# The maxima of a matrix-memory recurrence: rows through DRAM and a GpSimd mask instead of two wide products

## The chip, the cores and the metric

The kernel runs on one core of one Trainium2 chip. The core has TensorE (PE, matrix products), VectorE (DVE), ScalarE (ACT), GpSimd (POOL), and SyncE (SP), which here issues every DMA of the kernel. The time is device time in microseconds of one launch. The kernel before takes 2779.44 us (median of three runs, 2777.0 to 2782.29).

## The reference

One layer of a streaming encoder over 2048 tokens with 1024 features, all in 32-bit floats:

```
xn = RMSNorm(x);  proj = xn @ w_in
A = band attention, 8 heads of 64, a chunk of 64 tokens sees itself and 8 chunks to its left
M = matrix-memory recurrence (mLSTM), 4 heads of 128
y = sigmoid(ga) * (A @ w_att) + sigmoid(gm) * (M @ w_mlstm);  x = x + y @ w_out
x = x + relu(RMSNorm(x) @ w_up)^2 @ w_down;  out = RMSNorm(x)
```

The change is in M. For each head there is a log forget gate, summed to `b_t`, an input gate `i_s`, and a running maximum `m_t` that keeps the exponentials in range. Inside a chunk the output of token t weighs the values of the tokens s up to t by

```
D[t, s] = exp(b_t - b_s + i_s - m_t)   for s <= t, else 0
num_t = sum_s (q_t . k_s) D[t, s] v_s + (what the memory carried so far gives)
```

With `u_s = i_s - b_s` and `mt_t = m_t - b_t` the weight is `exp(u_s - mt_t)`: one number of the key's token, one of the query's token. The kernel needs it as a matrix with s over the 128 partitions and t over the columns, so `u` is one number per partition, and `mt` must be there as the same row in every partition, together with a mask for s > t.

## The kernel before, in words

The tokens are in four blocks of 512 (`NB`), each four tiles of 128 (`NT`). A block keeps features over partitions and its 512 tokens along the columns. The large products, input projections, the two projections of A and M, and the feed-forward part, run at 128x512 with operands split in a high and a low part, three products for one (`mm3` at L642, or L727 and L755, where blocks of a product are combined Strassen-like). Everything that does not fit into SBUF goes through DRAM tensors: q, k, v, the recurrence's inputs (`mfar`, `mvfar`), its results (`mixd`), gates and partial sums.

Buffers come from pools: 28 `r` (128x2x512), 16 `ctx` and 6 `tmp` (both 128x516), eight PSUM banks, and a few more. The order of the work is made in two steps when the kernel is built. First, `Flow` runs each piece of work as a thread that asks for buffers, waits for events, and asks for time on an engine (`yield "pe", 440`); the thread that can start earliest by a model of costs goes next. The large products are one thread of their own, `dense`, with the lowest priority. Then `Order` takes all instructions with their dependences, simulates them again with costs and margins of its own, and fixes the sequence on each of the five queues. No instruction passes another one on its queue on the chip.

A block's recurrence goes through these places:

- `gates_rest` (L1500): small operations on 128x16 tiles, a column for each tile and head. A cumulative sum and a running maximum (made on 16 rows, after a transpose) give `u`, `mt` and the factors `ex`. At the end (L1585 to L1592) `mt` is transposed, tile by tile, into a bank as rows of 512 tokens, and ScalarE and VectorE keep it in `mtt` as a rounded part in rows 0 to 3 and a remainder in rows 32 to 35. This sets the event `gates`.
- `recurrence_far` (L1596): takes the buffers of a head (two heads may be under way, `N_REC`), and starts `load_rec` (k, q and the values from DRAM) and `rec_head`.
- `rec_head` (L1662): two wide products into one bank. The first (L1670) multiplies a 16-bit identity by a 16-bit mask and so writes the mask, -1e30 for s > t, under all four tiles. The second (L1671) adds `-mt`, the high and the low row, in every partition. Then four exponentials on ScalarE (L1675) add `u` and give the weights `w`. Next the keys are transposed (L1682) and scaled (L1686), q and k multiplied (L1693), and the product multiplied into `w` on VectorE (L1695). Four tiles in turn then give the outputs (L1707 to L1709) and bring the memory forward (L1712). A norm (its root on GpSimd, L1729), transposes (L1742) and the output gate end the head, and its result is stored.

There are four blocks with four heads each, 16 heads. GpSimd also fills the corners of attention's bias tiles (L1324, L1325) and finishes eight output gates (L1659). Rows that go through DRAM into all partitions exist already for the norms: `row_out` (L1117) transposes 128x4 numbers, copies them and stores 512 numbers; `row_in` (L1131) reads them with a partition step of zero, 256 KB.

Of the kernel before, what the change touches and what calls it, by code (L numbers as in the profile page):

```python
# [30 lines left out]
P = 128  # L31
D = 1024
S = 2048
T = 512
# [178 lines left out]
def act_ns(n, ps=False, ap=0):  # L213
    return (51 if ps else 93) + 0.834 * n + 93 * ap
# [158 lines left out]
class Layer:  # L373
# [8 lines left out]
    def make_tiles(self, pool, psum):  # L382
# [14 lines left out]
        self.ones = f32("ones", 2)  # L397
        self.identb = pool.tile([P, P], BF16, name="identb")
        self.maskb = pool.tile([P, 1, P], BF16, name="maskb")
        self.gw = f32r("gw", KT, 40)  # L400
# [7 lines left out]
        self.cst = [f32(f"cst{h}", 129) for h in range(MH)]  # L408
        self.mtt = f32r("mtt", T)
        self.nsel = f32r("nsel", 8)  # L410
        self.cum = [pool.tile([16, 192], F32, name=f"cum{i}") for i in range(2)]
# [25 lines left out]
    def setup_late(self):  # L437
# [11 lines left out]
        nc.vector.tensor_sub(self.gw[:, :, 32:40], gwr, self.gw[:, :, 0:8].bitcast(F32))  # L449
        nc.vector.memset(raw[:, :512], 0.0)  # L450
        nc.vector.tensor_copy(self.mtt, raw[:, :512])
        fl.put(self.temp, raw)
# [7 lines left out]
        nc.vector.tensor_copy(self.bif[:, 1:, :], self.bif[:, 0:1, :].to_broadcast([P, NT - 1, 8]))  # L460
        nc.vector.tensor_copy(self.identb, self.ident)
# [1038 lines left out]
    def gates_rest(self, b):  # L1500
# [83 lines left out]
        V.tensor_scalar(ex[:, 2], ex[:, 2], C1, None, op0=ALU.mult)  # L1584
        yield "pe", 428  # L1585
        for c in range(NT):
            nc.tensor.transpose(bk[:MH, c * P:(c + 1) * P], sm["mt"][:, c * MH:(c + 1) * MH], self.ident)
# [27 lines left out]
    def load_rec(self, b, h):  # L1615
# [46 lines left out]
    def rec_head(self, b, h):  # L1662
# [4 lines left out]
        yield "wait", [B["gates"]]  # L1667
        (bk,) = yield "get", self.banks, 1
        yield "pe", 440
        mm(bk.rearrange("p (c t) -> p c t", c=NT), self.identb, self.maskb.to_broadcast([P, NT, P]), start=True, stop=False)  # L1670
        mm(bk, self.nsel[:, h:h + 1].to_broadcast([P, P]), self.mtt, start=False, stop=True)  # L1671
        for c in range(NT):
            n = c * MH + h
            yield "act", act_ns(128, True, 1)
            nc.scalar.activation(w[:, c * P:(c + 1) * P], bk[:, c * P:(c + 1) * P], AF.Exp,  # L1675
                                 bias=self.sm["u"][:, n:n + 1])
        fl.put(self.banks, bk)
        yield "wait", [B["qk_ev"][MH + h]]
# [4 lines left out]
        for c in range(NT):  # L1683
            n = c * MH + h
            yield "act", act_ns(128, True, 1)
            nc.scalar.mul(kt[:, c * P:(c + 1) * P], bk[:, c * P:(c + 1) * P], ex[:, 2, n:n + 1])  # L1686
        fl.put(self.banks, bk)
        yield "wait", [B["qk_ev"][h]]
        (bk,) = yield "get", self.banks, 1
# [767 lines left out]
    def build(self):  # L2457
# [16 lines left out]
        self.ud = f32d("u", 4, 7, 4, P, T)  # L2474
        self.rowd = {n: f32d("row" + n, T) for n in ("in1", "in2", "in3", "mid0", "mid1", "mid2", "mid3", "out0", "out1", "out2")}
        self.wi = 0
        self.y3 = [{}, {}]
# [16 lines left out]
        for b in range(NB):  # L2494
            self.blk.append(dict(
                xs=[], xg=[], vs={}, xs_ev=Event(), xn=E(KT), xs_done=E(KT), x2=E(KT), v_slots=Event(), v_ev=E(NT), v_spilt=E(NT),
                kq_ev=E(AH), q_ev=E(AH), k_ev=E(AH), k_spilt=E(AH), kq_all=Event(), head_done=E(AH),
                gates=Event(), mv_slots=Event(), mv_ev=E(NT), ctx={}, mvh={}, ctx_ev=E(MH), qk_ev=E(2 * MH), og_ev=E(MH),
                mix=[None] * 8, mix_ev=E(8), ga={}, ga_ev=E(8), xs_free=Event(), x_room=E(KT), mid=Event(), vo={}, vn={}, vp_ev=E(4), mvh_ev=E(MH), gf=Event(), rec_slots={}, heads_left=[2] * 4))
# [94 lines left out]
```

## Time and profile before

| | |
|---|---|
| runs, median | 2779.44 us (2777.0 to 2782.29) |
| the profiled execution | 2782.55 us, its span 2780.8 us |
| TensorE, weight loads | 99%, 82% of the span |
| VectorE, ScalarE, GpSimd | 74%, 54%, 2% |
| DMA | 678.64 MB, mean 244 GB/s |

The span runs from the first to the last instruction. A busy share of TensorE counts a product from its issue to its modelled end, and products overlap, so what one product takes from the next is the distance between their starts. In a group's row, the number after the bar is the time in which at least one instruction of the group ran, then the mean of one in ns, then the engine's idle time just before the group and what ended it. In a timeline's row come the start, the duration, the engine (with a q for its sequencer, which issues DMAs), the line, the operation and the tiles. A row of waits has the total, the number and the longest.

### The profile page before, as it was taken

Reading aid. Unit: us, or ns where it says so; the run is one execution under the profiler, and the core shown is the slowest. Engines: PE = TensorE matmul, PEld = TensorE weight load, DVE = VectorE, ACT = ScalarE, POOL = GpSimd, SP = SyncE. Lnnn points to the kernel's source line nnn. Section 1 sums busy time; section 2 is a strip of 40 time slices with the busy share of each in tenths; the row PEclk is TensorE's granted clock in tenths of the full one; section 3 lists DMA queues with packets and bytes.
Section 4 is the critical chain, followed back from the end, with each engine's and each line's share of the span. In section 5 each row is a group of like instructions: output and inputs, shape, how many; then the busy total and the mean of one; then the engine's idle time right before and its main releaser. Section 6 shows DMA issues by size and latency. Waiting matters only on the chain.

```text
span 2780.8 us, 38634 instructions
## 1 busy us (share of the span) xinstructions
PE 2754.7 (99%) x13018; PEld 2288.4 (82%) x13018; DVE 2055.0 (74%) x3776; ACT 1493.2 (54%) x2608; POOL 52.6 (2%) x100
## 2 busy tenths in 40 slices
PE   9999999999999999999999999999999999999998
PEld 7888888888778888888888888888887888888887
DVE  7696789758995866886676688789888656555565
ACT  5564576544453535575556556566436655554443
POOL 0000001000000000000000000000000000000000
PEclk9999999999999999999999999999999999999999
DMA  7958759768764677588877887787877667776574
GB/s 267 294 190 283 230 164 310 248 223 314 261 206 171 235 255 257 194 273 325 288 281 269 286 245 232 231 256 255 248 251 261 208 222 263 239 238 220 190 227 151
DMA packets 329046, 678.64 MB, mean 244 GB/s; under 512 B 36840, under 2 KB 67728, under 8 KB 328848
## 3 DMA queue, kind: packets, MB, share of 16 engines
q1 hardware_dynamic: 328848, 676.18, 73.3%
q8 instruction: 102, 1.67, 0.2%
q14 instruction: 96, 0.79, 0.1%
HBM read 472.59 MB, written 203.44 MB: 243 GB/s over the span
## 4 chain that ended last, share of the span: by engine, by line
PE 88%; DVE 4%; DMA 4%; issue 2%; ACT 1%; SPq 0%; POOLq 0%; POOL 0%; DVEq 0%; ACTq 0%
PE bank L727 41%; PE bank L644 12%; PE bank L645 11%; PE bank L646 11%; PE bank L1415 2%; PE bank L1388 2%; PE bank L755 2%; PE bank L1446 2%; DVE wsp L585 1%; DMA ctx<-in_xt 1%; DMA qfar<-ctx 1%; PE bank L1707 1%; PE bank L1709 1%; PE bank L1708 1%; PE bank L1693 0%
## 5 line engine op out<-in xcount | busy, mean ns | idle before, releaser
L727 PE MATMUL bank<-r,wsp 128*128 128x512 f32 x5544 | 1266.4, 390 | 2.9 <-DVE ctx L2088 1.5
L727 PEld LDWEIGHTS bank<-r,wsp 128*128 128x128 f32 x5544 | 1037.5, 188 | 225.4 <-DVE ctx L1874 4.2
L585 DVE TENSOR_TENSOR wsp<-wraw,wsp 128x1024 fp32r<-128x1024 f32 x459 | 560.5, 1221 | 352.9 <-ACT wsp L583 343.2
L583 ACT CAST wsp<-wraw 128x1024 fp32r<-128x1024 f32 x459 | 482.1, 1051 | 449.5 <-PE bank L727 202.9
L644 PE MATMUL bank<-r,wsp 128*128 128x512 f32 x1472 | 586.0, 398 | 2.8 <-ACT r L1224 2.8
L645 PE MATMUL bank<-r,wsp 128*128 128x512 f32 x1472 | 574.8, 391 | 0.2 <-DVE r L1229 0.2
L646 PE MATMUL bank<-r,wsp 128*128 128x512 f32 x1472 | 574.8, 391 | 0.0
L646 PEld LDWEIGHTS bank<-r,wsp 128*128 128x128 f32 x1472 | 276.2, 188 | 58.8
L644 PEld LDWEIGHTS bank<-r,wsp 128*128 128x128 f32 x1472 | 276.7, 188 | 54.2 <-ACT r L1224 3.1
L645 PEld LDWEIGHTS bank<-r,wsp 128*128 128x128 f32 x1472 | 277.0, 188 | 50.5 <-DVE r L1229 0.5
L1874 DVE TENSOR_TENSOR ctx<-bank,ctx 128x512 f32<-128x512 f32 x186 | 127.0, 687 | 91.6 <-PE bank L727 91.4
L1229 DVE TENSOR_TENSOR r<-r 128x512 fp32r<-128x512 f32 x248 | 163.7, 686 | 27.3 <-ACT r L1224 26.3
L1224 ACT CAST r<-r 128x512 fp32r<-128x512 f32 x248 | 147.5, 624 | 57.1 <-DMA r<-u 53.3
L1866 ACT COPY ctx<-bank 128x512 f32<-128x512 f32 x186 | 107.8, 581 | 66.7 <-PE bank L727 65.2
L1430 ACT ACTIVATE sc<-sc,scs 128x640 f32<-128x640 f32 (+4 forms) x128 | 97.4, 762 | 73.3 <-DVE scs L1427 63.0
L2205 ACT ACTIVATE ctx<-ctx 128x512 f32<-128x512 f32 x96 | 60.6, 631 | 103.1 <-DVE ctx L1874 103.1
L1451 DVE TENSOR_TENSOR r<-bank,r 128x512 fp32r<-128x512 f32 (+1 forms) x168 | 96.9, 595 | 17.4 <-ACT r L1449 16.6
L1449 ACT CAST r<-bank 128x512 fp32r<-128x512 f32 (+1 forms) x168 | 81.5, 517 | 48.7 <-PE bank L1446 45.6
L1421 DVE CUSTOM_DVE_ANT_0 sc<-bank,bias 128x320 f32<-128x320 f32 (+3 forms) x240 | 103.4, 461 | 5.5 <-PE bank L1415 5.0
L1388 PE MATMUL bank<-r,r 128*128 128x512 f32 x336 | 95.3, 365 | 1.3 <-DVE r L1451 1.2
L602 DVE TENSOR_TENSOR wraw<-wraw,wraw 128x1024 f32<-128x1024 f32 x76 | 92.8, 1223 | 2.0
L552 DVE TENSOR_TENSOR ctx<-ctx,ctx 128x512 f32<-128x512 f32 x112 | 76.2, 686 | 13.8 <-DMA ctx<-in_wf 9.7
(258 smaller groups left out, 2721.3 us busy)
## 6 DMA issues: line engine op xcount, KB each, us to landing
wraw<-in_wf SPq DMA_DIRECT2D x178, 512.0 KB, 4.3
wraw<-wsum SPq DMA_DIRECT2D x136, 512.0 KB, 3.9
r<-u SPq DMA_DIRECT2D x224, 256.0 KB, 4.4
wraw<-in_w SPq DMA_DIRECT2D x88, 512.0 KB, 5.2
u<-ctx SPq DMA_DIRECT2D x128, 256.0 KB, 2.8
ctx<-in_wf SPq DMA_DIRECT2D x112, 256.0 KB, 4.2
wsum<-ctx SPq DMA_DIRECT2D x112, 256.0 KB, 3.8
u<-tmp SPq DMA_DIRECT2D x96, 256.0 KB, 3.5
```

What stands on the lines that cost most here:

```text
L583: nc.scalar.copy(w[:, 0], raw)
L585: nc.vector.tensor_sub(w[:, 1], raw, w[:, 0].bitcast(F32))
L644: mm(ps, lh, rh, start=first, stop=False)
L645: mm(ps, lh, rl, start=False, stop=False)
L646: mm(ps, ll, rh, start=False, stop=last)
L727: mm(ps, wv[:, x, k, n], a[:, y], start=new and k == 0 and x == y == 0, stop=k == 3 and x == 1, skip_group_check=True)
L1224: self.nc.scalar.copy(dst[:, 0], src)
L1229: self.nc.vector.tensor_sub(dst[:, 1], src, dst[:, 0].bitcast(F32))
L1388: nc.tensor.matmul(acc[:, :, c0:c0 + w], st, sl[:, :, o:o + w], start=n == 0, stop=n == total - 1)
L1421: nc.vector.tensor_tensor_reduce(out=e[:, x * w:x * w + w], in0=bks[x][:, :w], in1=br[:, j0 + x * w:j0 + x * w + w], op0=ALU.add, op1=ALU. ...
L1866: nc.scalar.copy(t[:, o:o + 512], ps)
L1874: nc.vector.tensor_add(t[:, o:o + 512], ps, t[:, o:o + 512])
```

## The change

`mt` no longer goes to `mtt`. VectorE copies it with heads ahead of tiles, one transpose makes 16 rows of 128, ScalarE copies these to SBUF, and SyncE stores them in a DRAM tensor `rowm` of the block. A new thread for each head, `row_rec`, reads the head's 512 numbers back into all partitions of `w`, and GpSimd adds `later`, a 128x128 mask of 0 and 1e30, under each of the four tiles. `rec_head` drops the two products, their bank, and the exponentials in front; it makes the exponentials behind the scaled keys, in place in `w`, with scale -1. `mtt`, `nsel`, `identb` and `maskb` go, and a seventh `tmp` buffer comes in.

```diff
-        self.temp = Pool([f32(f"tmp{i}", 516) for i in range(6)])
+        self.temp = Pool([f32(f"tmp{i}", 516) for i in range(7)])
...
-        nc.vector.tensor_scalar(self.maskb[:, 0], self.tri, 1.0, -NEG, op0=ALU.subtract, op1=ALU.mult)
-        nc.vector.tensor_scalar(self.nsel, self.sel, -1.0, None, op0=ALU.mult)
+        nc.vector.tensor_scalar(self.later[:, 0], self.tri, NEG, -NEG, op0=ALU.mult, op1=ALU.add)
...
-        yield "pe", 428
-        for c in range(NT):
-            nc.tensor.transpose(bk[:MH, c * P:(c + 1) * P], sm["mt"][:, c * MH:(c + 1) * MH], self.ident)
-        yield "act", act_ns(512, True)
-        nc.scalar.copy(self.mtt[:MH], bk[:MH])
-        yield "dve", dve_ns(512)
-        yield "dve", 85
-        V.tensor_sub(self.mtt[32:32 + MH], bk[:MH], self.mtt[:MH].bitcast(F32))
+        yield "dve", 85
+        V.tensor_copy(p.rearrange("p (m c) -> p m c", c=NT), v4("mt").rearrange("p c m -> p m c"))
+        yield "pe", 110
+        nc.tensor.transpose(bk[:16, 384:512], p, self.ident)
+        yield "act", act_ns(P, True)
+        nc.scalar.copy(z[:, 64:], bk[:16, 384:512])
         fl.put(self.banks, bk)
+        yield "sp", 900, 2000
+        nc.sync.dma_start(self.rowm[b].ap(), z[:, 64:])
         fl.set(B["gates"])
...
             fl.spawn(self.load_rec(b, h), 1)
+            fl.spawn(self.row_rec(b, h, B["ctx"][h][3]), 1)
             fl.spawn(self.rec_head(b, h), 1)
...
+    def row_rec(self, b, h, w):
+        fl, nc, B = self.fl, self.nc, self.blk[b]
+        yield "wait", [B["gates"]]
+        yield "sp", 900, 2000
+        nc.sync.dma_start(w[:, :T], bass.AP(self.rowm[b], h * T, [[0, P], [1, T]]))
+        yield "pool", 730
+        w4 = w[:, :T].rearrange("p (c t) -> p c t", c=NT)
+        nc.gpsimd.tensor_tensor(w4, w4, self.later.to_broadcast([P, NT, P]), op=ALU.add)
+        fl.set(B["row_ev"][h])
...
         yield "wait", [B["gates"]]
-        (bk,) = yield "get", self.banks, 1
-        yield "pe", 440
-        mm(bk.rearrange("p (c t) -> p c t", c=NT), self.identb, self.maskb.to_broadcast([P, NT, P]), start=True, stop=False)
-        mm(bk, self.nsel[:, h:h + 1].to_broadcast([P, P]), self.mtt, start=False, stop=True)
-        for c in range(NT):
-            n = c * MH + h
-            yield "act", act_ns(128, True, 1)
-            nc.scalar.activation(w[:, c * P:(c + 1) * P], bk[:, c * P:(c + 1) * P], AF.Exp,
-                                 bias=self.sm["u"][:, n:n + 1])
-        fl.put(self.banks, bk)
         yield "wait", [B["qk_ev"][MH + h]]
...
             nc.scalar.mul(kt[:, c * P:(c + 1) * P], bk[:, c * P:(c + 1) * P], ex[:, 2, n:n + 1])
         fl.put(self.banks, bk)
+        yield "wait", [B["row_ev"][h]]
+        for c in range(NT):
+            n = c * MH + h
+            yield "act", act_ns(128, False, 1)
+            nc.scalar.activation(w[:, c * P:(c + 1) * P], w[:, c * P:(c + 1) * P], AF.Exp, scale=-1.0,
+                                 bias=self.sm["u"][:, n:n + 1])
         yield "wait", [B["qk_ev"][h]]
```

More of the change, by code (lines that the diff above doesn't have):

```diff
@@ L397, in make_tiles @@
         self.ones = f32("ones", 2)
-        self.identb = pool.tile([P, P], BF16, name="identb")
-        self.maskb = pool.tile([P, 1, P], BF16, name="maskb")
+        self.later = f32("later", 1, P)
         self.gw = f32r("gw", KT, 40)
@@ L408, in make_tiles @@
         self.cst = [f32(f"cst{h}", 129) for h in range(MH)]
-        self.mtt = f32r("mtt", T)
-        self.nsel = f32r("nsel", 8)
         self.cum = [pool.tile([16, 192], F32, name=f"cum{i}") for i in range(2)]
@@ L2475, in build @@
         self.rowd = {n: f32d("row" + n, T) for n in ("in1", "in2", "in3", "mid0", "mid1", "mid2", "mid3", "out0", "out1", "out2")}
+        self.rowm = [f32d(f"rowm{b}", 16, P) for b in range(NB)]
         self.wi = 0
@@ L2497, in build @@
                 kq_ev=E(AH), q_ev=E(AH), k_ev=E(AH), k_spilt=E(AH), kq_all=Event(), head_done=E(AH),
-                gates=Event(), mv_slots=Event(), mv_ev=E(NT), ctx={}, mvh={}, ctx_ev=E(MH), qk_ev=E(2 * MH), og_ev=E(MH),
+                gates=Event(), mv_slots=Event(), mv_ev=E(NT), ctx={}, mvh={}, ctx_ev=E(MH), qk_ev=E(2 * MH), row_ev=E(MH), og_ev=E(MH),
                 mix=[None] * 8, mix_ev=E(8), ga={}, ga_ev=E(8), xs_free=Event(), x_room=E(KT), mid=Event(), vo={}, vn={}, vp_ev=E(4), mvh_ev=E(MH), gf=Event(), rec_slots={}, heads_left=[2] * 4))
```

3 lines of the change are left out of this document (removed).

## The prediction

> **What bounds the kernel now.** I read the page first (span, busy shares, granted clock, DMA queue), then the waits of TensorE, then its timeline at both ends and around the lines that the change touches.
>
> ```profile
> span 2780.8 us, 38634 instructions
> PE 2754.7 (99%) x13018; PEld 2288.4 (82%) x13018; DVE 2055.0 (74%) x3776; ACT 1493.2 (54%) x2608; POOL 52.6 (2%) x100
> PEclk9999999999999999999999999999999999999999
> q1 hardware_dynamic: 328848, 676.18, 73.3%
> ```
>
> TensorE (PE) is busy for 99% of the span at an undiminished clock. VectorE (DVE), ScalarE (ACT) and the DMA queue have a quarter or more left, and GpSimd (POOL) is all but unused. A high busy share can hide stalls, so I looked at what TensorE waited for:
>
> ```profile
> PE bank L644 <- ACT r L1180: 6.7, 1, 6.7
> PE bank L644 <- ACT r L1224: 2.8, 1, 2.8
> PE bank L1707 <- DMA r<-mvfar: 0.9, 1, 0.9
> ...
> 2770.67 1.13 PE L2435 MATMUL bank<-const,ctx 128*128 128x128 f32 x7
> ```
>
> The first wait, 6.7 us, is the start of the program. The last products end at 2770.67 + 1.13 = 2771.8 us, so 9.0 us are the tail. Of the 2780.8 - 2754.7 = 26.1 us without TensorE work, 26.1 - 6.7 - 9.0 = 10.4 us lie inside, the longest of them 2.8 us. In this kernel a TensorE instruction that disappears is time, unless something new makes TensorE wait.
>
> **The change part by part.** First the two wide products a head.
>
> ```profile
> L1671 PE MATMUL bank<-mtt,nsel 128*128 128x512 f32 x16 | 9.0, 583 | 0.0
> L1670 PE MATMUL bank<-maskb,identb 128*128 128x512 bf16 x16 | 6.2, 388 | 0.0
> ...
> 69.01 0.39 PE L646 MATMUL bank<-r,wsp 128*128 128x512 f32 x1
> 69.24 0.39 PE L1670 MATMUL bank<-maskb,identb 128*128 128x512 bf16 x1
> 69.28 0.58 PE L1671 MATMUL bank<-mtt,nsel 128*128 128x512 f32 x1
> 69.70 0.39 PE L1670 MATMUL bank<-maskb,identb 128*128 128x512 bf16 x1
> ...
> 70.16 0.39 PE L644 MATMUL bank<-r,wsp 128*128 128x512 f32 x1
> ```
>
> The groups' busy columns, 9.0 + 6.2 = 15.2 us, are not the saving: they hold each product from issue to modelled end, and products overlap (the ordinary one at 69.01 is listed with 0.39 us, yet the next starts after 0.23). What TensorE gives up is the distance between starts. Two heads run from 69.24 to 70.16, 0.92 us, so 0.46 us a head, and 16 heads give 7.4 us. I take starts because the neighbours are packed; the busy columns would be right only if TensorE did one product at a time, which these rows exclude.
>
> The maxima are also turned differently: four transposes of four columns a block become one of sixteen.
>
> ```profile
> 65.14 0.39 PE L646 MATMUL bank<-r,wsp 128*128 128x512 f32 x1
> 65.37 0.60 PE L1587 MATMUL bank<-const,g_mt 128*4 128x128 f32 x4
> ...
> 66.04 0.39 PE L645 MATMUL bank<-r,wsp 128*128 128x512 f32 x1
> ...
> 55.55 0.39 PE L646 MATMUL bank<-wsp,r 128*128 128x512 f32 x1
> 55.78 0.27 PE L1541 MATMUL bank<-const,g_u 128*16 128x128 f32 x1
> ...
> 56.12 0.39 PE L645 MATMUL bank<-wsp,r 128*128 128x512 f32 x1
> ```
>
> From the product before (65.14) to the second one after (66.04) are 0.90 us; two ordinary steps of 0.23 leave 0.44 for four transposes. L1541 has the shape of the new one: 0.57 less 0.46 is 0.11. Each block saves 0.33, four blocks 1.3 us. Together TensorE sheds 7.4 + 1.3 = 8.7 us.
>
> Now what is added. The rows below are the nearest to each step: a row read back from DRAM into all partitions (L1133, 256 KB, as here), a short row's copy and store (L1125, L1128), the only 128x512 GpSimd operation (L1659, one input where the new add has two), the k and q loads of a head (L1625), and an exponential from a bank (L1675) beside an activation from SBUF (L1761).
>
> ```profile
> L1125 ACT COPY tmp<-bank x10: 237/242/255, 180.7 to 2742.2; 4x128 f32<-4x128 f32 x10
> L1128 SPq DMA_DIRECT2D rowmid<-tmp x4: 265/270/305, 1358.7 to 2279.7; - x4
> L1133 SPq DMA_DIRECT2D tmp<-rowmid x8: 319/354/747, 1621.8 to 2688.3; - x8
> DMA to landing us min/median/max: 3.2/4.1/7.5
> ...
> L1659 POOL TENSOR_SCALAR ctx<-ctx,ghead x8: 902/1596/2022, 194.3 to 453.3; 128x512 f32<-128x512 f32 x8
> ...
> L1625 SPq DMA_DIRECT2D r<-mfar x32: 319/382/830, 135.5 to 1808.1; - x32
> DMA to landing us min/median/max: 3.3/6.0/8.2
> ...
> L1675 ACT ACTIVATE ctx<-bank,g_u 128x128 f32<-128x128 f32 x64 | 18.4, 378 | 5.8 <-PE bank L1671 5.8
> ...
> L1761 ACT ACTIVATE tmp<-tmp 128x128 f32<-128x128 f32 x64 | 19.9, 310 | 16.6 <-DVE tmp L1757 13.2 <-DVE ctx L2242 2.8 <-DVE r L1229 0.3
> ```
>
> *Queues.* SyncE issues 4 stores and 16 loads more, 4 x 0.27 + 16 x 0.35 = 6.7 us in all, and the loads add 16 x 0.26 = 4.2 MB to 676 MB (0.6%) on a queue at 73%. I cost both at nothing: TensorE's waits name DMA once, for 0.9 us. Without that cover each load would cost its issue, 0.35 us. The load behind a fresh store must wait until the store has landed, and whatever SyncE holds behind it (mostly weight and operand loads) waits too; by the landings of L1133 that is 3.2 to 7.5 us, four times at most, less what the planner puts between.
>
> *GpSimd.* 16 adds of 0.9 to 2.0 us, 14 to 32 us on an engine with 52.6 us of work. Queued behind them are the bias memsets of attention and the root of a head's norm; both have idle time before them. An add may also slow VectorE (third rival).
>
> *ScalarE.* 64 exponentials move behind the turned keys and read SBUF: at most 64 x (378 - 310) ns = 4.4 us less work, off the path, so nothing.
>
> *The setup and the spare buffer.* Some small VectorE work before 30 us goes. The seventh temporary buffer can only let loads start earlier; at best it removes part of the 10.4 us inside, and the new written order may equally make other waits. I take zero, with 10.4 us to either side as bounds.
>
> *The head's own chain* is the one term that can hurt. Before, the products needed only the gates; now a head needs load, add and exponentials before its weights (L1695), and TensorE needs these at L1707. A tight head, and (last two rows) the first heads of the last block, which start from fresh gates:
>
> ```profile
> 207.14 0.38 SPq L1625 DMA_DIRECT2D r<-mfar  x1
> 211.34 1.73 POOL L1659 TENSOR_SCALAR ctx<-ctx,ghead 128x512 f32<-128x512 f32 x1 [7.08 <-ACT ctx L1656]
> 214.90 1.14 ACT L1686 ACTIVATE ctx<-bank,g_ex 128x128 f32<-128x128 f32 x4
> 216.19 0.68 DVE L1695 SCALAR_TENSOR_TENSOR ctx<-bank,ctx 128x512 f32<-128x512 f32 x1
> 218.67 0.38 PE L1707 MATMUL bank<-r,ctx 128*128 128x129 f32 x2
> ...
> 1779.94 0.60 PE L1587 MATMUL bank<-const,g_mt 128*4 128x128 f32 x4
> ...
> 1796.49 0.41 PE L1707 MATMUL bank<-r,ctx 128*128 128x129 f32 x2
> ```
>
> Issued just behind the keys at 207.5, the row lands at 211.6 (4.1), waits for the operation on GpSimd to 213.1, is added by 214.7 (1.6), and its exponentials follow the scaled keys at 216.0 and take 1.2: 217.2. The weights then start 1.0 us later than now and end at 217.9, 0.8 us ahead of L1707. With the longest landing, 7.5, the row comes at 215.0, the add ends at 216.6, the exponentials at 217.8 and the weights at 218.5, still ahead by 0.2. With the longest add as well (2.0) TensorE waits 0.2 us, and where the other head's add stands ahead on GpSimd, 2.0 more. From fresh gates: turned at 1780.5, copy 0.24, store issue 0.27 and landing 4.1 (no row gives a short store's landing; I use the load's), load 0.35 and 4.1, add 1.6, exponentials of two heads 2.5, weights 0.7, so 1794.4, 2.1 us ahead of L1707. The bounds a head are thus 0 and some 2.2 us; I take 0.9 us in all, the one wait for a DMA at L1707 that TensorE shows among 16 such loads, since the planner lays other products in between in the same way.
>
> The sum on the profiled execution, which took 2782.55 us (its span 2780.8): 2782.55 - 8.7 + 0.9 = 2774.7. That execution lies 3.1 us above the median of the runs, 2779.44, so the forecast for the median is 2779.44 - 7.8 = 2771.6 us, 0.28% less.
>
> **The rivals.** *The order is planned anew and the gain is swallowed.* Every instruction behind the first gates is laid out again. If the 10.4 us inside become 10.4 + 7, the time is 2779.44 - 8.7 + 7 = 2777.7, no difference that can be told. For it: the inner idle is already so small that a new order is likelier to add to it than to take away. Against: the other work stays what it is, and the planner that now leaves 10.4 us of holes is the one that lays it out again.
>
> *Rows come late (the other side).* The place is L1707 (and L1693 ahead of it); the price is up to 2.2 us a head. It decides from 8.7 / 16 = 0.54 us a head on: at 1.2 us on average, 16 x 1.2 = 19 us, the time is 2779.44 - 8.7 + 19 = 2790. For it: load, add and exponentials now stand in a row, behind queues that hold other work. Against: 32 loads at L1625 that take up to 8.2 us never show in TensorE's waits, and 16 at L1707 once.
>
> *The adds hold VectorE off.*
>
> ```profile
> L1229 DVE TENSOR_TENSOR r<-r 128x512 fp32r<-128x512 f32 x248 | 163.7, 686 | 27.3 <-ACT r L1224 26.3
> ...
> 438.29 1.75 POOL L1659 TENSOR_SCALAR ctx<-ctx,ghead 128x512 f32<-128x512 f32 x1 [3.09 <-ACT ctx L1656]
> ...
> 439.48 1.10 DVE L1229 TENSOR_TENSOR r<-tmp,r 128x512 fp32r<-128x512 f32 x1
> ```
>
> This split, 0.69 us in the mean, took 1.10 beside the GpSimd operation that runs from 438.29 to 440.04. If TensorE waited for a whole add of 2.0 us each time, 32 us, the time would be 2779.44 - 8.7 + 32 = 2803. Against: VectorE is idle for a quarter of the span and all of TensorE's inner idle time is 10.4 us, so I expect 0.4 us of VectorE delay for an add, hidden. [...]
>
> **How the numbers follow.** About 0.2%, 5.6 us, is what a measurement of this kernel can tell from no change. The forecast, TensorE time saved and all or nearly all kept, has 0.62, with a range of its own from 2762 (8.7 saved and most of the inner idle gone) to 2773.8. Swallowed: 0.20. Late rows: 0.14; VectorE held off: 0.04. So faster 0.62, same 0.20, slower 0.18. The range for 8 in 10 leaves out the best tenth, and the worse half of the slower cases: 2762 to 2788.
>
> **What would show it.** TensorE's instructions fall by 32 + 12 to 12974 and its span time with them; L1670 and L1671 vanish, and no new wait on ScalarE's exponentials, on the weights of L1695 or on DMA appears in its waits with more than 1 us in total. GpSimd gains 16 operations of 0.9 to 2.2 us, DMA 4.2 MB. I am wrong if TensorE's idle time inside exceeds 10.4 us by over 3, above all at L1707 or L1693, or if bank or weight waits on VectorE grow near the adds.

## The result, and the profile after

The changed kernel takes 2794.92 us (median of six runs, 2790.74 to 2798.68) beside 2779.51 us of the kernel before (six runs). The ratio is 1.0056, with a 95% interval from 1.0045 to 1.0066: 0.56% slower, where 0.28% faster was forecast.

The head of the page of the changed kernel (span; busy time, share and instructions of each engine; DMA queue):

```profile
span 2792.7 us, 38602 instructions
PE 2753.1 (99%) x12974; PEld 2288.6 (82%) x12974; DVE 2055.9 (74%) x3772; ACT 1494.5 (54%) x2608; POOL 74.6 (3%) x116
q1 hardware_dynamic: 331280, 680.41, 72.2%
```

TensorE has the 44 instructions less that were forecast, GpSimd its 16 more, the queue its 4.2 MB more, at 72.2% of its time where it was 73.3%. But the span less TensorE's busy time, 26.1 us before, is 2792.7 - 2753.1 = 39.6 us now, and the busy time fell by only 1.6 us where 8.7 were removed. So 13.5 us of idle time are new. The waits of TensorE show where they lie (what waited, for what; us in total, times, longest):

```profile
PE bank L1677 <- DMA r<-mfar: 7.0, 4, 2.4
PE bank L637 <- ACT r L1173: 6.4, 1, 6.4
PE bank L637 <- ACT r L1217: 5.0, 1, 5.0
...
PE bank L1708 <- DVE ctx L1696: 1.9, 1, 1.9
...
PE bank L1708 <- POOL ctx L1664: 1.1, 1, 1.1
PE bank L1694 <- DVE r L1444: 0.9, 1, 0.9
...
PE bank L1694 <- DMA r<-mfar: 0.5, 1, 0.5
PE bank L1708 <- issue: 0.5, 1, 0.5
```

L1677 are the transposes of the keys (L1682 before), L1694 the product of q and k, L1708 the outputs, L637 the large products and L1217 a cast of one of their operands (L1224 before). The start of the program, 6.4 us, is all but as it was (6.7). New are 7.0 us for key loads; the cast costs 5.0 in place of 2.8; the outputs cost 1.9 + 0.5 + 1.1 = 3.5 in place of 0.9. The 1.1 us are put down to an output gate's operation on GpSimd (L1664), but the weights of L1696 end 0.04 us behind it and may be what was waited for. L1694 costs 1.4 in place of 0.2. This makes 7.0 + 2.2 + 2.6 + 1.2 = 13.0 of the 13.5 us.

The other part of the loss is in the granted clock. Four stretches of 100 us by engine, of the changed kernel (the columns: stretch, us, busy time of PE, PEld, DVE, ACT and POOL, the granted clock, DMA share, GB/s):

```profile
100.00:200.00 100.00, 97.16 (x530) 82.71 (x529) 85.16 (x265) 64.73 (x159) 6.23 (x16) 0.98 0.75 230
400.00:500.00 100.00, 95.36 (x511) 81.12 (x511) 87.81 (x211) 69.87 (x165) 13.34 (x10) 0.98 0.75 249
1500.00:1600.00 100.00, 94.98 (x455) 79.64 (x455) 63.03 (x129) 56.00 (x105) 4.34 (x5) 0.98 0.94 314
1800.00:1900.00 100.00, 97.20 (x522) 82.69 (x521) 84.38 (x222) 56.31 (x132) 7.30 (x13) 0.98 0.85 256
```

and of the kernel before:

```profile
100.00:200.00 100.00, 98.30 (x552) 83.67 (x552) 87.29 (x277) 66.09 (x165) 5.81 (x17) 1.00 0.71 216
400.00:500.00 100.00, 99.01 (x521) 83.48 (x520) 90.55 (x203) 71.26 (x169) 13.07 (x9) 1.00 0.80 270
1500.00:1600.00 100.00, 96.94 (x474) 80.93 (x473) 61.63 (x133) 54.63 (x106) 2.37 (x3) 1.00 0.92 299
1800.00:1900.00 100.00, 100.00 (x558) 86.32 (x557) 86.59 (x235) 60.23 (x146) 7.76 (x10) 1.00 0.83 255
```

The four stretches hold 94.25 - 84.70 = 9.55 us more without TensorE work than before (394.25 busy in the sum before, 384.70 now), and in each of them the clock falls from 1.00 to 0.98. The record of the granted clock in the trace says what 0.98 is: it is halved for 3.413 us once in each, at 144.5, 465.35, 1564.44 and 1871.64 us. The timeline of TensorE around the first (start, duration, idle time before and what ended it in brackets):

```profile
141.41 0.40 PE L637 MATMUL bank<-r,wsp 128*128 128x512 f32 x1
143.85 0.66 PE L1677 MATMUL bank<-const,r 128*128 128x128 f32 x4 [2.05 <-DMA r<-mfar]
...
145.06 0.63 PE L637 MATMUL bank<-r,wsp 128*128 128x512 f32 x1
145.49 0.63 PE L638 MATMUL bank<-r,wsp 128*128 128x512 f32 x1
145.91 0.63 PE L639 MATMUL bank<-r,wsp 128*128 128x512 f32 x1
```

TensorE waits 2.05 us for a key load, and right behind the hole the products start 0.43 us apart, not 0.23. A busy engine at half the clock counts as busy, which is why the busy column hid it. With TensorE busy through it, each stretch loses half of 3.413 us, an estimate of 4 x 1.7 = 6.8 us. The profiled executions now add up: TensorE's busy time without that loss is 2753.1 - 6.8 = 2746.3, 8.4 less than the 2754.7 before (the forecast said 8.7); idle time adds 13.5 and the clock 6.8; -8.4 + 6.8 + 13.5 = 11.9 us, which is 2792.7 - 2780.8. The medians lie 15.4 us apart, because the profiled execution of the kernel before took 3.0 us more than its median; what those 3 us are, these traces don't show.

Why the key load is late there: SyncE's timeline of the changed kernel, the load of head 0 of the first block,

```profile
138.80 0.38 SPq L1619 DMA_DIRECT2D r<-mfar  x1
```

and of the kernel before,

```profile
135.48 0.38 SPq L1625 DMA_DIRECT2D r<-mfar  x1
```

with TensorE's transposes of these keys before:

```profile
145.77 0.66 PE L1682 MATMUL bank<-const,r 128*128 128x128 f32 x4
```

Before, 10.3 us lay between issue and use. Now TensorE is ready at 141.8, 3.0 us behind the issue, and the load lands some 5 us behind it. The loads of k and q of the changed kernel together (landing times, and who waited):

```profile
L1619 SPq DMA_DIRECT2D r<-mfar x32: 319/383/857, 138.8 to 1884.9; - x32
...
  PE bank L1677: 7.0, 4
...
DMA to landing us min/median/max: 2.6/6.0/7.8
```

The last planning step, `Order`, reckons such a load done 1.4 + 0.65 + 1.1 = 3.15 us after its issue if no other load stands ahead (`REACH`, the transfer of 256 KB, `LAND`); measured are 6.0 in the median, as in the kernel before. The loads didn't become slower; here TensorE asks for one sooner after its issue. The planner asks for the keys' transposes about when it believes the load to be there.

### The profile page after: what moved, and what is told of

It is laid out like the page before. It is cut to its first block, busy times and chain, and to the rows that moved or that the text cites. A ratio compares the mean times of both kernels' runs of the same rounds, so it can differ in the third digit from the quotient of the medians.

```text
span 2792.7 us, 38602 instructions
## 1 busy us (share of the span) xinstructions
PE 2753.1 (99%) x12974; PEld 2288.6 (82%) x12974; DVE 2055.9 (74%) x3772; ACT 1494.5 (54%) x2608; POOL 74.6 (3%) x116
## 3 DMA queue, kind: packets, MB, share of 16 engines
q1 hardware_dynamic: 331280, 680.41, 72.2%
## 4 chain that ended last, share of the span: by engine, by line
PE 86%; DMA 5%; DVE 4%; issue 2%; ACT 1%; SPq 0%; POOL 0%; POOLq 0%; DVEq 0%; ACTq 0%
PE bank L720 41%; PE bank L637 11%; PE bank L638 11%; PE bank L639 11%; PE bank L748 2%; PE bank L1381 2%; PE bank L1408 2%; PE bank L1439 2%; DMA r<-mfar 1%; DVE wsp L578 1%; DMA ctx<-rowm 1%; DMA ctx<-in_wf 1%; DVE ctx L2046 0%; PE bank L1708 0%; DMA wsum<-ctx 0%
## 5 line engine op out<-in xcount | busy, mean ns | idle before, releaser
L720 PE MATMUL bank<-r,wsp 128*128 128x512 f32 x5544 | 1265.6, 390 | 1.8 <-DVE ctx L2089 0.8
L720 PEld LDWEIGHTS bank<-r,wsp 128*128 128x128 f32 x5544 | 1038.0, 188 | 223.4 <-DVE ctx L1875 5.0
L637 PE MATMUL bank<-r,wsp 128*128 128x512 f32 x1472 | 587.7, 400 | 5.0 <-ACT r L1217 5.0
L638 PE MATMUL bank<-r,wsp 128*128 128x512 f32 x1472 | 576.0, 391 | 0.3 <-DVE r L1222 0.3
L637 PEld LDWEIGHTS bank<-r,wsp 128*128 128x128 f32 x1472 | 277.8, 189 | 56.6 <-ACT r L1217 5.3
L638 PEld LDWEIGHTS bank<-r,wsp 128*128 128x128 f32 x1472 | 277.7, 189 | 50.5 <-DVE r L1222 0.7
L1217 ACT CAST r<-r 128x512 fp32r<-128x512 f32 x248 | 148.1, 622 | 54.1 <-DMA r<-u 48.0
L1408 PE MATMUL bank<-r,r 128*128 128x320 f32 (+3 forms) x480 | 87.2, 306 | 0.0
```

The lines of the kernel that those rows point to most:

```text
L637: mm(ps, lh, rh, start=first, stop=False)
L638: mm(ps, lh, rl, start=False, stop=False)
L720: mm(ps, wv[:, x, k, n], a[:, y], start=new and k == 0 and x == y == 0, stop=k == 3 and x == 1, skip_group_check=True)
L1217: self.nc.scalar.copy(dst[:, 0], src)
L1408: nc.tensor.matmul(bks[x][:, :w], q[:, y, i * P:(i + 1) * P], kf[:, f * P + x * w:f * P + x * w + w], start=y == 0, stop=y == 1)
```

## The experiments

The theory formed from these traces, "keys uncovered": the two products and their exponentials stood at the front of a head and gave the key load time to land. The rivals: "row path" (store, load, add and exponentials come too late for weights and outputs), "new order" (any other written order is worse by chance), and "buffer" (the seventh temporary changes the order for the worse). All medians below stand beside 2778.6 to 2779.2 us of the kernel before in the same sessions.

**One part at a time.** The keys' transposes and scaling of the changed kernel behind the row's exponentials:

```diff
+        (wait for the row; the four exponentials)
         (wait for the keys; their four transposes and scalings)
-        (wait for the row; the four exponentials)
```

> The changed kernel with the keys' transposes and their scaling moved behind the row's exponentials in each head. Exposed keys (the key load lost the products and exponentials that gave it time to land): TensorE's waits on the key load, 7.0 us in the changed kernel, fall below 1 us, a half-clock stretch or two goes with them, time near 2785. Late rows (the row's load and add come too late for the weights): nothing gained, 2795 or more. New order (the planner's holes are redrawn by any edit): anywhere from 2775 to 2800, with the waits at other lines.

2796.42 us, ratio 1.0067 [1.0052, 1.0082], no better. The wait for key loads stays, 6.0 us, 5.3 of it once: the planner now issued that load itself later, at 448.34 us. A place in the written thread doesn't fix how long a load has.

The changed kernel without the row's load and add (the row's store stays; the exponentials read the mask alone, with another bias, so the weights are not the reference's):

```diff
-            fl.spawn(self.row_rec(b, h, B["ctx"][h][3]), 1)
...
-        yield "wait", [B["row_ev"][h]]
...
-            nc.scalar.activation(w[:, c * P:(c + 1) * P], w[:, c * P:(c + 1) * P], AF.Exp, scale=-1.0,
-                                 bias=self.sm["u"][:, n:n + 1])
+            nc.scalar.activation(w[:, c * P:(c + 1) * P], self.later[:, 0], AF.Exp, scale=-1.0,
+                                 bias=self.sm["bc"][:, n:n + 1])
```

> The changed kernel without the row's loads and without the adds on GpSimd: the exponentials read the mask alone, with a finite number per partition as bias, so the weights are not the reference's. Exposed keys: TensorE still waits some 7 us for key loads, time 2790 or more. Late rows: the waits at the first output product (3.5 us) and what follows from them go, time 2785 to 2789. New order: no set place, 2775 to 2800.

2785.40 us (seven runs, 2779.20 to 2789.45), ratio 1.0022 [1.0009, 1.0035]. Its waits of TensorE:

```profile
PE bank L1676 <- DMA r<-mfar: 7.4, 5, 3.4
PE bank L637 <- ACT r L1173: 6.2, 1, 6.2
PE bank L1439 <- DVE sc L1427: 2.6, 2, 1.7
PE bank L637 <- ACT r L1217: 2.0, 1, 2.0
```

With no row to wait for, the keys (L1676 here) wait as in the changed kernel, and the time is 14.6 us above the 2770.8 that it would have if all of the 8.7 were kept. The row path is worth 2794.92 - 2785.40 = 9.5 us, the other order included that comes with it; it is not the whole.

The kernel before with the keys ahead of the two products and their exponentials; no work is removed or added:

```diff
+        (wait for the keys; their four transposes and scalings)
         (bank; the two products; the four exponentials)
-        (wait for the keys; their four transposes and scalings)
```

> The kernel before with the keys' transposes and scaling moved ahead of the two wide products and their exponentials. Exposed keys: TensorE waits 5 to 7 us for key loads where it waited for none, time 2786 to 2790. Late rows: no row path here, so 2779.5. New order: 2770 to 2795 with waits anywhere.

2792.24 us, ratio 1.0048 [1.0031, 1.0064]: 13.7 us for trading two steps of a head. The waits of TensorE:

```profile
PE bank L644 <- ACT r L1224: 4.4, 1, 4.4
PE bank L1672 <- DMA r<-mfar: 2.9, 2, 2.1
PE bank L1693 <- DMA r<-mfar: 2.3, 1, 2.3
PE bank L1709 <- DVE cst L1712: 2.1, 2, 1.2
```

L1672 are the keys here. Loads of keys and queries cost 5.2 us, the cast 4.4, and the clock is halved for 13.7 us in all, at 231, 463 and 1566 us.

The changed kernel with six temporary buffers (`range(7)` back to `range(6)`):

> The changed kernel with six temporary buffers as before. If the seventh buffer's earlier loads are what crowds the others, time falls toward 2780. Exposed keys and late rows: 2793 to 2797 with the same waits. New order: anywhere from 2775 to 2800.

2795.88 us, ratio 1.0061 [1.0045, 1.0077]. Taking the spare buffer away wins nothing back; that rival falls.

**Only the planner's estimates.** Two numbers of the kernel before that change no instruction, only the order: the estimate of the two products, and that of a norm's root.

```diff
-        yield "pe", 440
+        yield "pe", 460
```

> The kernel before, not one instruction added or removed: only the planner's estimate for the two wide products of a head is 460 in place of 440 ns, which lays most of TensorE's sequence out anew. New order (the kernel before holds an unusually tight sequence, and any new one has more holes): 2784 to 2796, with new waits of TensorE and half-clock stretches between 100 and 500 us and between 1500 and 1900 us. Exposed keys and late rows: no cause for any change, 2777 to 2782.

2779.03 us, ratio 1.0001 [0.9991, 1.0010], though in the traces 1762 of TensorE's 13018 places are taken by another line's instruction than before. From its waits:

```profile
PE bank L644 <- ACT r L1180: 6.6, 1, 6.6
PE bank L644 <- ACT r L1224: 3.2, 1, 3.2
...
PE bank L1707 <- DMA r<-mvfar: 0.5, 1, 0.5
```

```diff
-        yield "pool", 960
+        yield "pool", 980
```

> The kernel before, with the planner's estimate for the root in a head's norm 980 in place of 960 ns and nothing else. New order: 2782 to 2796. Exposed keys and late rows: 2777 to 2782.

2781.19 us, ratio 1.0007 [0.9996, 1.0017]. So by the medians a new order as such costs 0.3 and 2.5 us in these two draws. The second isn't harmless throughout: its profiled execution, at 2790.93 us the slowest of its ten, waits 2.4 us for key loads and has three stretches at half the clock.

In the changed kernel, four estimates that were too short. The add on GpSimd (the number is ns):

```diff
-        yield "pool", 730
+        yield "pool", 1400
```

> The changed kernel, with the planner's estimate for the add on GpSimd 1400 in place of 730 ns (measured 1262 to 2372, median 1377). Late rows: the weights are planned nearer to their true time, the waits at the first output product (3.5 us) shrink, 2788 to 2792. Exposed keys: no change, 2793 to 2797. New order: another draw, 2775 to 2800.

2790.72 us, ratio 1.0047 [1.0031, 1.0062]: some 4 us better, with 6.1 us of key waits.

```diff
-    REACH, LAND, FAR = 1400.0, 1100.0, 2500.0
+    REACH, LAND, FAR = 1400.0, 3500.0, 2500.0
```

> The changed kernel, with the time that the planner gives a DMA from its last byte to its use at 3500 in place of 1100 ns, so that a 256 KB load is planned at 5.5 us (median landing of the key loads 6.0). If TensorE's new waits come from loads that the planner expects too early, the waits on key loads fall below 1 us and the time to 2772 to 2782. If any order has such holes, 2785 to 2797.

2790.84 us, ratio 1.0046 [1.0029, 1.0062]. Told that every load lands 2.4 us later, the planner cuts the key waits to 0.6 us; in their place the outputs wait 4.2 us for a value load and a blocked product (L720) 4.0 us for a cast.

The first planning step's latency of the loads of k and q, in the changed kernel:

```diff
-            yield "sp", 900, 2000
+            yield "sp", 900, 5000
```

> The changed kernel, with the first planning step told that the loads of a head's keys and queries take 5000 in place of 2000 ns, so that the keys' transposes stand later in TensorE's sequence. Exposed keys: the waits on key loads (7.0 us in the changed kernel) fall below 1.5 us and a half-clock stretch or two goes, 2783 to 2788. Late rows: 2793 to 2797. Any order with the keys in front has such holes: 2790 to 2797.

2789.14 us, ratio 1.0035 [1.0022, 1.0048], key waits 5.2 us and 2.0 at q·k. The same with the row's load at 5000 and the add at 1400:

> As the run before, and the row's load planned at 5000 in place of 2000 ns and its add at 1400 in place of 730 ns. Exposed keys and late rows both at work: key waits and waits at the first output product together below 2 us, 2773 to 2780, at or ahead of the kernel before. If only one counts: 2783 to 2790. If neither: 2790 to 2797.

2787.19 us, ratio 1.0031 [1.0020, 1.0043], key waits 4.9 us and 2.1 at q·k. The kernel without the row path, with 5000 for k and q:

> The changed kernel without row load and add (weights not the reference's), with the key and query loads planned at 5000 ns. Exposed keys: of the 15.4 us between 2770 (the kernel before less 8.7 us of products) and the 2785.4 without rows, most goes: 2770 to 2777. Otherwise: 2783 to 2788.

2786.61 us, ratio 1.0025 [1.0011, 1.0040], key waits 8.0 us and 2.0 at q·k. And the kernel before with it:

> The kernel before with the key and query loads planned at 5000 ns. It has no waits on key loads to lose, so exposed keys expect no gain: 2777 to 2783. If the larger figure helps for another reason, it helps here too: 2768 to 2775.

2786.94 us, ratio 1.0029 [1.0019, 1.0038]: worse by 8 us. A truer number in the first step alone hardly moves the loads (the first head's key load of the changed kernel is issued 3.9 us ahead of a free TensorE in place of 3.0), since the second step writes the order by its own number, and it can turn a good order into a worse one.

**The cover.** The kernel without the row path, now with the exponentials in front of the keys, as before: this is the kernel before less its products, newly planned.

> The changed kernel without row load and add, as in the earlier run (weights not the reference's), with the exponentials moved back to the front of the head, ahead of the keys, as in the kernel before; what is missing against the kernel before is the products and little else. If the keys' place behind the exponentials is what covered their load: 2769 to 2774, no waits on key loads. If the products themselves at the front cover it: 2783 to 2788, with the same waits on key loads as with the keys first (7.4 us).

2789.81 us, ratio 1.0040 [1.0024, 1.0055], with 4.2 us at q·k and 2.2 at the keys for loads. So the exponentials' place alone isn't the cover.

Then the second planning step was told the measured landing, 3000 ns more, for these loads and those of the values (`mvfar`) alone, in both its due times and its simulation (in the kernel before without `rowm`):

```diff
+    def slow(self, k):
+        src = self.operands(self.ins[k].ins)[0].tensor.name
+        return 3000.0 if src.startswith(('mfar', 'mvfar', 'rowm')) else 0.0
...
-            less = self.dur[k] + (self.FAR if self.eng[k] == "SP" else 0.0)
+            less = self.dur[k] + (self.FAR + self.slow(k) if self.eng[k] == "SP" else 0.0)
...
-                end = queue + self.LAND
+                end = queue + self.LAND + self.slow(k)
```

> The changed kernel, with the second planning step (which fixes each queue) told that the loads of keys, queries and rows take 3000 ns longer than other loads, both where it ranks what is due and where it simulates. Exposed keys: waits on key loads below 1 us, time 2780 to 2787. Late rows as well: the waits at the first output product go too, 2775 to 2782. If every order without the products in front has such holes: 2788 to 2797.

2785.23 us, ratio 1.0021 [1.0011, 1.0030]: 9.7 us won back, and the best that the changed kernel reached. The waits of TensorE:

```profile
PE bank L641 <- ACT r L1177: 5.9, 1, 5.9
PE bank L1712 <- DMA r<-mvfar: 5.4, 1, 5.4
PE bank L641 <- ACT r L1221: 5.0, 1, 5.0
```

No key wait is left. What is left is one value load (L1712 are the outputs), issued at 454.62 us and wanted at 455.7, and the cast. The clock is halved at each of these two holes, for 6.8 us from 459 and for 3.4 us from 1558, and once more for 3.4 us at 981.6, behind a hole of 1.98 us in the blocked products.

> The kernel before with the same 3000 ns for the loads of keys and queries. It has no waits there to lose: 2777 to 2785. If the figure helps for another reason: 2768 to 2775.

The kernel before, told the same: 2785.08 us, ratio 1.0015 [1.0006, 1.0025], again 4.2 us for a value load, 3.7 us for the cast. So the planner's error isn't simply a defect whose repair helps: the order of before, made with the wrong landing time, is better by 6 us than the one made with the right one.

**The products' time or their place in the plan.** The last three separate what the theory had run together. First, the kernel before with products of 16 columns, charged by the planner as 512, so that its order stays all but the same:

```diff
-            return max(110.0, 13.7 + self.count(outs[0]) / 2.4)
+            return max(110.0, 13.7 + (512 if any(a.tensor.name in ("maskb", "mtt") for a in ins) else self.count(outs[0])) / 2.4)
...
-        mm(bk.rearrange("p (c t) -> p c t", c=NT), self.identb, self.maskb.to_broadcast([P, NT, P]), start=True, stop=False)
-        mm(bk, self.nsel[:, h:h + 1].to_broadcast([P, P]), self.mtt, start=False, stop=True)
+        (the same two, on the last 4 columns of each tile)
...
             (the exponentials read these 4 columns 32 times)
```

> The kernel before, written in very nearly its own order (about a hundred of some 13000 TensorE lines trade places), but the two products of a head are 16 columns wide in place of 512 while the planner still charges them as 512; the exponentials read those 16 columns repeated, so the weights are not the reference's. TensorE sheds 0.46 less two short products of some 0.06 us, thus 0.34 us a head, 5.4 us in all, and nothing else is moved. Theory (the time at the head's front is the cover of the key load, and 0.46 us a head is too little to uncover a load that was early): in this order the keys are wanted up to 10 us after their issue, so nearly all is kept, 2774 to 2776 us, and no wait of the keys' transposes above 1 us; what costs in the changed kernel is the other order that the planner writes. Rival (each product's own 0.46 us is the cover): waits for the key loads of 2 us or more appear and the time is 2780 to 2786 us.

2778.79 us (ten runs), ratio 1.0001 [0.9992, 1.0011]. Its head of the page and, in the timeline, two heads' products:

```profile
span 2773.5 us, 38632 instructions
PE 2749.4 (99%) x13018; PEld 2286.3 (82%) x13018; DVE 2055.1 (74%) x3776; ACT 1493.0 (54%) x2608; POOL 51.0 (2%) x100
```

```profile
68.93 0.18 PE L1670 MATMUL bank<-maskb,identb 128*128 128x16 bf16 x1
...
69.23 0.48 PE L644 MATMUL bank<-r,wsp 128*128 128x512 f32 x1
69.55 0.39 PE L645 MATMUL bank<-r,wsp 128*128 128x512 f32 x1
```

In the traces 143 of TensorE's 13018 places hold another line's instruction than before. Two heads take 0.30 us in place of 0.92, 0.075 us a short product (the 0.06 of the expectation was an estimate that no earlier run shows), and the product behind them starts its successor 0.09 later, so TensorE sheds (0.62 - 0.09) / 2 = 0.27 us a head, 4.2 us in all. No key wait comes of it (0.3 us in all), and the span less the busy time is 24.1 us: the rival of this run, that the products' own time is the cover, falls, and with it "keys uncovered" in its first form. The profiled execution, 2775.25 us, is the fastest of the ten, so it doesn't show that the time is kept. In the median it isn't: 0.2 us are won of 4.2, and the interval allows from 2.2 us won to 3.1 lost. The mean of the granted clocks of these runs is 0.9979, beside 0.9985 of the runs of the kernel before, 0.0006 x 2779 = 1.7 us; the other 2.3 us stay unexplained. So even in its own order this kernel wasn't shown to keep what is taken from TensorE at this place.

Second, the changed kernel (with six temporaries) with two wide products on constants again at the front of each head:

```diff
+        (bk,) = yield "get", self.banks, 1
+        yield "pe", 440
+        for _ in range(2):
+            mm(bk.rearrange("p (c t) -> p c t", c=NT), self.identb, self.maskb.to_broadcast([P, NT, P]), start=True, stop=True)
+        yield "act", act_ns(128, True, 1)
+        nc.scalar.copy(w[:, 512:513], bk[:, :1])
+        fl.put(self.banks, bk)
         yield "wait", [B["qk_ev"][MH + h]]
```

> The changed kernel with six temporary buffers and two products 128x512 again at the front of each head, on constants, whose result nobody needs (one column is copied away). TensorE has 7.4 us more work than in the run with six temporary buffers (2795.9). Theory (the front products keep the planner from drawing the keys forward): the key waits of 5.7 us shrink below 2 us and the half-clock stretches behind them go, so the added work is paid back, 2787 to 2796 us. Rival (only the row path costs time): the work adds up, 2800 to 2804 us, with key waits as they are.

2796.59 us, ratio 1.0062 [1.0047, 1.0077]. The waits of TensorE:

```profile
PE bank L1719 <- DVE ctx L1707: 6.4, 2, 5.8
PE bank L641 <- ACT r L1177: 6.3, 1, 6.3
PE bank L1688 <- DMA r<-mfar: 2.2, 2, 1.7
```

With 7 us more work the time is that of the run without it (2795.88): key waits fall from 5.7 to 2.2 us (2.1 us more, once, in front of the same transposes are put down to a cast), but the outputs (L1719) now wait 5.8 us for the weights of L1707 at 1547 us, and that hole halves the clock for 6.8 us. Third, the same with products of 16 columns, charged as 512:

> As the run with the two added products, but these are 16 columns wide and still charged as 512 by the planner, so its order is nearly that run's with some 5.4 us less work on TensorE. Theory: 5 us below that run, 2781 to 2791 us. Rival (the products' real duration is the cover): no gain against that run, or a loss, with waits of the keys' transposes that it doesn't have.

2794.33 us, ratio 1.0055 [1.0039, 1.0071], which can't be told from the run before it. Key waits are 5.8 us, the outputs wait 6.7 us for the memory carried forward. The order is that of the run before it in all but 135 of 13006 places, so these key waits, 5.8 after 2.2 (4.3 with the cast), and the missing gain are what its rival expected: in this order the products' own time may cover some of the loads, as it didn't in the order of the kernel before.

No version was shown to be faster than the kernel before.

## Why the prediction was wrong, point by point

- **TensorE sheds 8.7 us: right.** 44 instructions went, and the busy time without the halved clock fell by 8.4 us. That one pair agrees partly by luck, since this time moves with the order too: from 2750.8 to 2754.7 us in six profiled orders of the kernel before, from 2742.1 to 2747.2 in eight of the changed one with its row path. The means, 2752.8 and 2744.6, lie 8.2 us apart.
- **"In this kernel a TensorE instruction that disappears is time, unless something new makes TensorE wait": the step that failed.** The escape clause was not priced: the new written order was put at zero ("I take zero, with 10.4 us to either side as bounds"), and the waits were looked for in the head's chain alone. In the profiled executions 13.5 us of new waits and 6.8 us of halved clock came against the 8.4 that were shed, and the idle time inside grew from 10.4 to 39.6 - 6.4 - 9.0 = 24.2 us, the prediction's own sign of being wrong. The first half of the sentence isn't shown either: with the products thinned in the old order, no new key wait came, and yet the interval allows at most 2.2 of 4.2 us won.
- **The head's chain "is the one term that can hurt", 0.9 us in all: wrong in place and size.** The sum followed the row through load, add and exponentials, and asked what TensorE waits for at L1707 and L1693. There it found 0.9; measured are 3.5 us at the outputs and 1.4 at q·k. The largest item, 7.0 us for key loads at the transposes, was not on the list: that the head's first TensorE instruction is now one that needs a load was not seen, and "32 loads at L1625 that take up to 8.2 us never show in TensorE's waits" was taken as a property of the loads, where it was one of the order. Without any row path 2785.40 us are left, 14.6 above the full gain.
- **The rivals.** "The order is planned anew and the gain is swallowed" came nearest: it had 7 us more idle time and 2777.7 us, where 13.5 us came, and the clock on top. The reason against it, that the same planner lays the work out again, carried no weight: with equal work other orders of the kernel before cost 0.3, 2.5, 5.9, 7.9 and 13.7 us. "Rows come late" has the right side, but its place holds 4.9 us in all. What "The adds hold VectorE off" rests on, a VectorE instruction that takes longer beside a GpSimd operation, is there, and hidden, as forecast. A split beside an add in the changed kernel:

```profile
1507.96 1.76 POOL L1634 TENSOR_TENSOR ctx<-ctx,later 128x512 f32<-128x512 f32 x1 [125.00 <-DMA ctx<-rowm]
...
1508.77 1.49 DVE L1222 TENSOR_TENSOR r<-r 128x512 fp32r<-128x512 f32 x1 [0.21 <-ACT r L1217]
```

  It takes 1.49 us where the mean is 0.70, 0.79 us more, and the add had 0.95 us left; in the prediction's own row it was 0.41 us more, with 0.56 us left. So in these two rows VectorE lost most of what was left. Summed over the 16 adds, the VectorE instructions beside them take some 5.5 us longer than the medians of their like, 0.34 us an add where 0.4 was forecast. Only 0.3 us of TensorE's waits name such a split (L638), far from the 32 us of this rival.
- **SyncE, DMA, ScalarE at nothing: the reason given didn't hold for DMA.** It was that TensorE's waits name DMA once, for 0.9 us; now they name it for 7.0 + 0.5 us. The queue isn't slower, the key loads land in 6.0 us in the median as before; the planner issues the first head's 3.3 us later, and TensorE wants it 4.0 us earlier (141.8 in place of 145.77).
- **GpSimd, 0.9 to 2.0 us an add: nearly right.** The adds of the changed kernel (shortest, median, longest in ns):

```profile
L1634 POOL TENSOR_TENSOR ctx<-ctx,later x16: 1262/1377/2372, 78.0 to 1898.4; 128x512 f32<-128x512 f32 x16
```

  The 1.6 us taken, from another operation (L1659), lie above the median of 1.38 us. The rows land later than forecast, 7.3 us in the median beside the 4.1 of the rows of the norms, and that lengthens the chain by 3.2 us where it is tight.
- **The spare buffer, zero: right** as far as four runs tell (2795.88 without it). The order, put at zero in the same term, was not.
- **The range** ended at 2788, below the prices of its own two slow rivals (2790 and 2803), and no term let a hole cost more than its length. In the changed kernel each of four holes had 3.413 us at half the clock at its end or behind it, by estimate 1.7 us more.

What stays open: of the 24 us between 2770.8 and 2794.9, telling the planner the landing times gave 9.7 back and taking the row path out gave 9.5, but both change the whole order and were not combined, so they are not a sum. Why the longest hole of every profiled order but that of the thin products in the kernel before (2.83 us in the kernel before, 3.0 to 6.9 in the others) ends near 455 to 468 us or near 1551 to 1565 us isn't settled. That the products' time is the cover is excluded for the order of the kernel before alone. What the runs agree on is that the order around the heads decides: no order that was moved there was faster, and trading two steps without any change of work cost 13.7 us.

## What to carry to other kernels

Before counting removed work as time, ask what the work stood in front of: list the first instruction behind it on the bounding engine and the time from issue to use of each load that this instruction needs, and compare it with the measured landing time (6.0 us here), not with the planner's (3.15 us). Where a program writes the order by estimates, a change of work is also a draw of a new order; run the kernel before with one harmless estimate changed, and with its steps traded, to see how wide that draw is. Read the record of the granted clock behind each hole of the bounding engine: here a hole of 2.05 us on TensorE, with the clock halved behind it, cost by estimate 1.7 us more.

## What the hardware showed

Holes on TensorE cost more than their length here where the clock was halved behind them, by estimate 1.7 us for each 3.413 us at half clock. In the profiled execution of the changed kernel the clock is halved for 3.413 us at the end of, or within 2 us behind, holes of 2.05 us (from 141.8 us), 2.36 us (461.2), 5.02 us (1559.7) and 1.94 us (1868.5). A hole of 2.83 us in the kernel before brought none; its timeline there:

```profile
1549.03 0.38 PE L1742 MATMUL bank<-const,tmp 128*128 128x128 f32 x2
1552.24 0.49 PE L644 MATMUL bank<-r,wsp 128*128 128x512 f32 x1 [2.83 <-ACT r L1224]
1552.96 0.50 PE L645 MATMUL bank<-r,wsp 128*128 128x512 f32 x1 [0.23 <-DVE r L1229]
```

The records of the clock sort the holes. In each profile every change of the clock lies on one grid with a step of 3.413 us: from 465.35 to 1564.44 us, for example, are 1099.09 us, 322 steps of 3.4133. In the changed kernel's profile the four steps at full clock that held 1.94 to 3.41 us of TensorE's idle time were each followed by a step at half clock; none of the other steps was, with up to 1.45 us there and 1.71 us in the kernel before. Counted so over all 20 profiles, of 16144 steps at full clock 40 held more than 1.91 us of idle time, and the next step was at half clock for each of the 40; with less it was so three times (1.54, 1.56 and 1.72 us). The hole of 2.83 us, from 1549.41 to 1552.24, lies across the boundary at 1551.1 us, 1.7 us on one side and 1.1 on the other, and no step at half clock followed.

So a hole of that size had half clock behind it in some places and not in another, and the granted clock differed from run to run: in the sessions of the experiments, 40 runs of the kernel before whose mean granted clock was 0.999 took 2777.8 us in the mean, 31 runs at 0.998 took 2780.7, and 9 at 0.997 took 2782.7. The differences between these three groups are about half of this kernel's scatter (of the variance of these 80 runs). The halved stretches ahead of TensorE's last product last 3.413 us or a multiple of it in all the profiles.
